# Moving the second layer's conditioning loads: two groups beside the end of the first layer's mixers, one beside the end of its FFN

## The chip, the cores and the metric

The kernel runs on one core of a Trainium2 chip. The metric is the device time of one execution in microseconds; lower is better. The engines that matter here are TensorE (PE), VectorE (DVE), ScalarE (ACT), GpSimd (POOL) and SyncE (SP), whose queue issues almost all DMAs. Every engine works through its own list of instructions in order and waits where an input or a buffer is not ready.

## The reference, cut to what matters

Two layers work on 256 context tokens and 256 latent tokens, each 1024 wide. The conditioning of a layer is one matrix product with a weight of 1024 x 6144 values:

```python
for li in range(DEPTH):                      # DEPTH = 2
    sh1, sc1, g1, sh2, sc2, g2 = split(silu(c) @ w_ada[li] + b_ada[li], 6)        # latent tokens
    sh1c, sc1c, g1c, ... = split(silu(c_ctx) @ w_ada[li] + b_ada[li], 6)          # context tokens
    p = split(modulate(x, sh1, sc1) @ w_in[li])            # input projection, 2700 columns
    mix = concat(window_attention(p), mamba2(p), diff_attention(p)) @ w_out[li]
    x = post_ln(ALPHA * x + g1 * mix)
    x = post_ln(ALPHA * x + g2 * ffn(modulate(x, sh2, sc2)))   # layer 0: SwiGLU, layer 1: 2 of 8 experts
    # context tokens: the same in layer 0; in layer 1 they only give keys, values and states
```

So of the second layer's six vectors, the first shift and scale are wanted before its input projection, the first gate and the second shift only at its output projection, and the second scale and gate after that.

## The kernel before, in words

The program is one stream of Python that emits instructions; a scheduler with its own timeline then fixes each engine's list. There are five stages: conditioning and mixers of layer 0 (to about 438 us), the FFN of layer 0 (to about 820 us), the mixers of layer 1 (to about 1086 us), routing, and the experts (from about 1120 us to the end).

**Conditioning.** `ada_group(L, g)` (from L289) computes a third of the six vectors: 2048 columns. It loads 16 pieces of 512 KB of `w_ada` (L248, called through `load_w`), and for each piece issues four matmuls of 128 x 32 by 128 x 256 (L311), which the trace records as eight, since each fp32 matmul counts twice. Below, such a piece with its matmuls is called a chunk. A group has two halves of eight chunks, and at the end of each half DVE adds the bias into the tile `rows` (L319). Group 0 then goes through two transposes into the modulation columns (L332); groups 1 and 2 write gate and shift rows to memory by DMAs in POOL's queue, `gscr<-rows` (L342).

**Buffers.** All weights outside the experts (`w_ada`, `w_in`, `w_out`, `ffn_w_down`, `ffn_w_gu`) go through one set of four buffers, the tile `raw` (`NRAW` = 4), and are issued by SP in list order. A weight that is not `w_ada` is split into a high part by ACT (`whi`, L254) and a low part by DVE or POOL (`wlo`, L255), three buffers each; its `raw` buffer is free after that. A `w_ada` buffer is free only when TensorE has read it.

**Mixers.** `mixers` weaves generators by weights and marks: the dense projection with `fill` blended into it (after `SKIP` pieces, `nfill` steps to a piece), then the output projection (`tail`); the attention streams; and the Mamba task `"S"`. A generator waits at `"?name"` until another one has yielded `"+name"`. The output projection of layer 0 is `tail0`: context tokens first, then latent tokens, `out_ab` with four sets of weights and `out_c` with two.

**Where the second layer's groups stand.** Group 0 follows the mixers of layer 0 (`for _ in ada_group(L1, 0): pass`). Groups 1 and 2 are the `fill` of the second layer's own mixers.

**End of the FFN.** The second half of the down projection has four parts, in the order `DN`: 512 columns for the context tokens, the other 512, then the same for the latent tokens. Each part takes five loads of 512 KB and one of 256 KB (tile `dn`). After a token group's second part come its layer norm, a store of the two token tiles to memory (`xscr<-xr`, L1186, in SP's queue), and the transposes `hT` that make the input of the next layer's projection (`tok` and `xbc` are the tiles of that projection).

Of the kernel before, what the change touches and what calls it, by code (L numbers as in the profile page):

```python
# [53 lines left out]
DN = ((0, CTX), (1, CTX), (0, LAT), (1, LAT))  # L54
SKIP = 11, 6
NRAW, NSPL, OT = 4, 3, 3
W1P, W2P, WCP, SYP, PRE, ADP, FUL = 1, 0, 1, 1, 1, (2, 2), 4
# [53 lines left out]
def kernel(ctx: ExitStack, tc: tile.TileContext, I, out: bass.AP):  # L111
# [57 lines left out]
    def mark(m):  # L169
        yield m  # L170
# [329 lines left out]

    def mixers(L, full_ctx, fill, tail):
        li = L.li
# [528 lines left out]
        for n in names:  # L1031
            if n == "/":
                streams.append([])
            else:
                streams[-1].append(n)
                todo.add(n)
        weave((1.0, chain(blend(dense_gen(), chain(*fill), nfill, SKIP[li]), tail)),
              *((wa[i] if type(wa) is tuple else wa, attention(n)) for i, n in enumerate(streams)), (ws, task("S")))

# [84 lines left out]

    def ffn(L, pp, done):
        li = L.li
# [27 lines left out]
        for half in range(2):  # L1154
# [8 lines left out]
            for c, tiles in ((0, (0, 1, 2, 3)), (1, (0, 1, 2, 3))) if half == 0 else DN:  # L1163
# [4 lines left out]
                for n in (2, 2, 2, 2, 2, 1):  # L1168
# [3 lines left out]
                    for t in tiles:  # L1172
                        ts_ = slice(t * 128, (t + 1) * 128)
                        mm3(pd[t], [(*(x[:, ts_] for x in act[f0 + i]), wh[:, i], wl[:, i], False) for i in range(n)],
                            f0 == 11 * half, f0 + n == 11 * half + 11)
                    f0 += n
                for t in tiles:
                    gt = gates[1 if t in CTX else 0]
                    tmp = L.pp.tile([128, 512], F, name="dtmp", tag="otmp", bufs=OT)
                    V.tensor_tensor(tmp, pd[t], gt[:, cs_], op=OP.mult)  # L1180
                    V.scalar_tensor_tensor(xs[t][:, cs_], xs[t][:, cs_], ALPHA if half == 0 else 1.0, tmp,
                                           op0=OP.mult, op1=OP.add)
                if half == 1 and c == 1:
                    for t in tiles:
                        post_ln(xs[t], g, b)
                        SP.dma_start(xscr[t * 128:(t + 1) * 128], xs[t])  # L1186
                    done(tiles)
# [509 lines left out]
    def tail0():  # L1697
# [3 lines left out]
        ns = {}  # L1701
        for tiles in TL0:
            yield from out_ab(L0, tiles, pp)
            for v in out_c(L0, tiles, pp):
# [13 lines left out]

    mixers(L0, True, [ada_group(L0, 1), ada_group(L0, 2)], tail0())
    for _ in ada_group(L1, 0):  # L1720
        pass
    with tc.tile_pool(name="ffn", bufs=1) as fp:
        ffn(L0, fp, lambda tiles: make_hT(L0.pp, L1.mod1, {t: layernorm(L0.pp, L0.xs, t) for t in tiles},
                                          tiles[0] // 2))
    post.close()
# [29 lines left out]

    mixers(L1, False, [ada_group(L1, 1), ada_group(L1, 2)], tail1())
    tail_ctx.close()
# [31 lines left out]
```

## Time and profile before

| | us |
|---|---|
| median of three runs (1867.45 to 1872.87) | 1867.92 |
| the profiled execution | 1867.13 |
| its span, first to last instruction | 1865.3 |
| PE busy, share of the span | 1712.7, 92% |
| DVE busy, share of the span | 1146.8, 61% |
| DMA, mean over the span | 234 GB/s |

The span is what the trace covers; 1.8 us of the execution lie around it. A busy PE is not a PE at its peak, since matmuls overlap and PE's clock is granted in steps. A share over the whole span says little here: the experts keep the DMA engines at 0.95 from 1120 us on, and the mixers leave them idle for tens of microseconds.

### The profile page before, as it was taken

To read this page: it belongs to the slowest core of one execution; us is meant where nothing else is said; L and a number is where in the kernel's file an instruction comes from. 1 tells how busy PE (TensorE), PEld (TensorE's weight loads), DVE (VectorE), ACT (ScalarE), POOL (GpSimd) and SP (SyncE) were. 2 spreads that over 40 slices of the span, in tenths; PEclk is the share of its full clock that TensorE was granted. 3 is DMA by queue.
4 is the path that set the end of the run, shared out by engine and by line. 5 is a ranking of instruction groups with operands and counts; after the bars stand their busy time and mean duration, and the time that the engine had idled before them with its cause. 6 is when DMAs were issued, how large, how long until landed. Compare 5 with 4: busy or idle time off the path is not lost.

```text
span 1865.3 us, 26243 instructions
## 1 busy us (share of the span) xinstructions
PE 1712.7 (92%) x9355; PEld 1262.9 (68%) x9355; DVE 1146.8 (61%) x2242; ACT 873.3 (47%) x1460; POOL 327.9 (18%) x254
## 2 busy tenths in 40 slices
PE   5889999788999999979989949999999999999995
PEld 2677667576888888857866723486458537888884
DVE  4773577768433333485777670487068408898987
ACT  3533546437322233345435721375157317777774
POOL 1221023354310222952232420000000000000000
PEclk8999999798999999998999969999999999999998
DMA  9237254158432332546672359999999999999991
GB/s 309 79 105 229 81 173 150 46 173 257 125 102 89 93 101 90 164 154 216 200 228 72 109 183 397 409 406 401 369 409 406 380 396 408 408 370 359 340 324 50
DMA packets 251002, 436.37 MB, mean 234 GB/s; under 512 B 15056, under 2 KB 166232, under 8 KB 250864
## 3 DMA queue, kind: packets, MB, share of 16 engines
q1 hardware_dynamic: 248944, 429.81, 65.1%
q0 software_dynamic: 1920, 4.81, 0.9%
q8 instruction: 76, 1.25, 0.3%
q14 instruction: 62, 0.51, 0.1%
HBM read 431.34 MB, written 3.23 MB: 233 GB/s over the span
## 4 chain that ended last, share of the span: by engine, by line
PE 75%; DMA 8%; DVE 8%; issue 3%; ACT 2%; POOL 1%; SPq 0%; DVEq 0%; ACTq 0%; POOLq 0%
PE mg L1365 6%; PE mu L1365 5%; PE mdn L1365 5%; PE gu L271 4%; PE gu L268 4%; PE gu L269 4%; DMA raw<-in_w_ada 4%; PE mg L1519 3%; PE mg L1354 3%; PE mu L1519 3%; PE mu L1354 3%; PE mdn L1354 3%; DMA mraw<-in_exp_w_down 2%; PE tok L268 2%; PE tok L271 2%
## 5 line engine op out<-in xcount | busy, mean ns | idle before, releaser
L1345 DVE TENSOR_TENSOR mwl<-mraw,mwh 128x1024 fp32r<-128x1024 f32 (+2 forms) x372 | 388.7, 1103 | 26.1 <-ACT mwh L1344 18.3
L1344 ACT ACTIVATE mwh<-mraw 128x1024 fp32r<-128x1024 f32 (+2 forms) x372 | 339.8, 965 | 84.0 <-DMA mraw<-in_exp_w_gu 45.6
L255 POOL TENSOR_TENSOR wlo<-raw,whi 128x1024 fp32r<-128x1024 f32 (+2 forms) x93 | 230.7, 2487 | 480.5 <-ACT whi L254 422.2
L254 ACT ACTIVATE whi<-raw 128x1024 fp32r<-128x1024 f32 (+2 forms) x168 | 168.3, 1004 | 239.1 <-PE dn L269 71.9
L255 DVE TENSOR_TENSOR wlo<-raw,whi 128x1024 fp32r<-128x1024 f32 (+2 forms) x75 | 88.3, 1178 | 144.2 <-ACT whi L254 142.4
L268 PE MATMUL gu<-HI,whi 128*128 128x512 f32 (+1 forms) x400 | 144.4, 369 | 2.3 <-ACT whi L254 2.3
L269 PE MATMUL gu<-LO,whi 128*128 128x512 f32 (+1 forms) x400 | 144.9, 369 | 0.0
L311 PE MATMUL ada<-raw,cT 128*32 128x256 f32 x768 | 74.8, 429 | 41.8 <-DMA raw<-in_w_ada 38.3
L268 PE MATMUL tok<-whi,HI 128*128 128x256 f32 (+2 forms) x400 | 108.0, 299 | 4.4 <-ACT xin L545 3.1
L269 PE MATMUL tok<-whi,LO 128*128 128x256 f32 (+2 forms) x400 | 105.5, 293 | 5.3 <-DVE LO L439 4.1
L271 PE MATMUL gu<-HI,wlo 128*128 128x512 f32 (+1 forms) x400 | 98.5, 367 | 0.0
L268 PEld LDWEIGHTS tok<-whi,HI 128*128 128x128 f32 x400 | 78.6, 197 | 13.5 <-issue 4.4
L268 PEld LDWEIGHTS gu<-HI,whi 128*128 128x128 f32 x400 | 75.9, 191 | 15.8 <-ACT whi L254 2.5
L269 PEld LDWEIGHTS gu<-LO,whi 128*128 128x128 f32 x400 | 76.2, 191 | 12.7
L269 PEld LDWEIGHTS tok<-whi,LO 128*128 128x128 f32 x400 | 78.5, 197 | 9.2 <-DVE LO L439 5.9
L271 PEld LDWEIGHTS gu<-HI,wlo 128*128 128x128 f32 x400 | 70.3, 188 | 12.9
L268 PE MATMUL dn<-whi,ah 128*128 128x512 f32 x176 | 70.2, 399 | 4.9 <-ACT whi L254 4.9
L1354 PE MATMUL mdn<-mwl,mah 128*128 128x512 f32 x220 | 72.8, 399 | 0.9 <-DVE mwl L1345 0.5
L1365 PE MATMUL mdn<-mwh,mah 128*128 128x512 f32 x220 | 73.5, 399 | 0.0
L1528 DVE TENSOR_TENSOR msl<-msl,mu 128x512 f32<-128x512 f32 (+1 forms) x9 | 5.8, 643 | 110.0 <-PE mu L1519 110.0
L271 PE MATMUL tok<-wlo,HI 128*128 128x256 f32 (+2 forms) x400 | 71.4, 296 | 1.9 <-DVE nw L222 1.9
L1365 PE MATMUL mdn<-mwh,mal 128*128 128x512 f32 x220 | 72.5, 394 | 0.0
(358 smaller groups left out, 3645.6 us busy)
## 6 DMA issues: line engine op xcount, KB each, us to landing
mraw<-in_exp_w_gu SPq DMA_DIRECT2D x128, 1024.0 KB, 12.4
mraw<-in_exp_w_down SPq DMA_DIRECT2D x87, 1024.0 KB, 14.5
mraw<-in_exp_w_gu SPq DMA_DIRECT2D x64, 768.0 KB, 11.4
raw<-in_w_ada SPq DMA_DIRECT2D x88, 512.0 KB, 5.4
raw<-in_ffn_w_gu SPq DMA_DIRECT2D x100, 256.0 KB, 3.3
raw<-in_w_in SPq DMA_DIRECT2D x38, 512.0 KB, 5.1
raw<-in_ffn_w_down SPq DMA_DIRECT2D x30, 512.0 KB, 3.5
E<-cscr POOLq DMA_DIRECT2D x12, 384.0 KB, 7.1
```

The costliest lines, as they stand in the source:

```text
L254: S.activation(hi, raw, AF.Copy)
L255: (eng or V).tensor_tensor(lo, raw, hi.bitcast(F), op=OP.subtract)
L268: T.matmul(o, ah, bh, start=start and i == 0, stop=False)
L269: T.matmul(o, *((ah, bl) if wa else (al, bh)), start=False, stop=False)
L271: T.matmul(o, *((al, bh) if wa else (ah, bl)), start=False, stop=stop and i == n - 1)
L311: T.matmul(pa[32 * j:32 * j + 32, hs], cT[:, k], w[j], start=(k == 0), stop=(k == KC - 1), tile_position=(0, 32 * j), skip_group_check=True)
L1344: S.activation(wh, raw, AF.Copy)
L1345: V.tensor_tensor(wl, raw, wh.bitcast(F), op=OP.subtract)
L1354: T.matmul(pc[:, :w], xh, wl[:, c * 512:c * 512 + w], start=False, stop=stop)
L1365: T.matmul(pc[:, :w], x, wh[:, c * 512:c * 512 + w], start=start and x is xh, stop=False)
L1519: T.matmul(p[hs, :n], Xf[:, kk, hs], raws[h][:, k, c * n:(c + 1) * n], start=kk == 0, stop=kk == KC - 1, skip_group_check=True)
L1528: V.tensor_tensor(sl[:, cs_], sl[:, cs_], p[:, :n], op=OP.mult)
```

## The change

`ada_group(L1, 0)` no longer stands alone after the first layer's mixers: groups 0 and 1 of the second layer are now a further generator woven into those mixers with weight 0.5, from the mark `late`, which `tail0` sets when it turns to the latent tokens. Group 2 becomes a side generator of `ffn`: one step (two chunks) after each of the five 512 KB loads of the last part of the down projection, and the rest, six chunks, before that part's layer norm. The second layer's mixers get an empty `fill`. The arithmetic is the same.

```diff
+WADA = 0.5
-    def mixers(L, full_ctx, fill, tail):
+    def mixers(L, full_ctx, fill, tail, aside=()):
...
-              *((wa[i] if type(wa) is tuple else wa, attention(n)) for i, n in enumerate(streams)), (ws, task("S")))
+              *((wa[i] if type(wa) is tuple else wa, attention(n)) for i, n in enumerate(streams)), (ws, task("S")),
+              *aside)
...
-    def ffn(L, pp, done):
+    def ffn(L, pp, done, side):
...
                     f0 += n
+                    if half == 1 and c == 1 and tiles == LAT and n == 2:
+                        next(side, None)
...
                 if half == 1 and c == 1:
+                    if tiles == LAT:
+                        for _ in side:
+                            pass
                     for t in tiles:
                         post_ln(xs[t], g, b)
...
         for tiles in TL0:
+            if tiles == LAT:
+                yield "+late"
             yield from out_ab(L0, tiles, pp)
...
-    mixers(L0, True, [ada_group(L0, 1), ada_group(L0, 2)], tail0())
-    for _ in ada_group(L1, 0):
-        pass
+
+    mixers(L0, True, [ada_group(L0, 1), ada_group(L0, 2)], tail0(),
+           [(WADA, chain(mark("?late"), ada_group(L1, 0), ada_group(L1, 1)))])
     with tc.tile_pool(name="ffn", bufs=1) as fp:
         ffn(L0, fp, lambda tiles: make_hT(L0.pp, L1.mod1, {t: layernorm(L0.pp, L0.xs, t) for t in tiles},
-                                          tiles[0] // 2))
+                                          tiles[0] // 2), ada_group(L1, 2))
...
-    mixers(L1, False, [ada_group(L1, 1), ada_group(L1, 2)], tail1())
+    mixers(L1, False, [], tail1())
```

The lists of the engines show where the chunks now stand. The first place is SP's list at the output projection of the first layer's latent tokens. Before, it holds the third and fourth set of `out_ab` weights and the two loads of `out_c`, with no `w_ada` among them:

```order
L248 DMA raw<-in_w_out 64x3x256 x2
L248 DMA raw<-in_w_out 128x256
L248 DMA raw<-in_w_out 128x2x256
L346 DMA bc<-gscr 128x1024
L248 DMA raw<-in_w_out 64x3x256 x2
L248 DMA raw<-in_w_out 128x256
L248 DMA raw<-in_w_out 128x2x256
L248 DMA raw<-in_w_out 128x2x512 x2
```

Now, from the end of the first set on:

```order
L249 DMA raw<-in_w_out 128x2x256
L249 DMA raw<-in_w_ada 128x4x256 x6
L249 DMA raw<-in_w_out 64x3x256 x2
L249 DMA raw<-in_w_out 128x256
L249 DMA raw<-in_w_out 128x2x256
L249 DMA raw<-in_w_ada 128x4x256 x3
L347 DMA bc<-gscr 128x1024
L249 DMA raw<-in_w_ada 128x4x256
L249 DMA raw<-in_w_out 64x3x256 x2
```

Six chunks have moved between the first and the second set, four between the second and the third. Before, all sixteen chunks of this stage follow the last `out_c` load; now there are thirty-two, of which eighteen stand ahead of the end of `out_c`.

The second place is SP's list at the last part of the FFN's down projection. Before:

```order
L248 DMA raw<-in_ffn_w_down 128x512
L248 DMA raw<-in_ffn_w_down 128x2x512 x3
L1186 DMA xscr<-xr 128x1024
L248 DMA raw<-in_ffn_w_down 128x2x512
L1186 DMA xscr<-xr 128x1024
L248 DMA raw<-in_ffn_w_down 128x2x512
L248 DMA raw<-in_ffn_w_down 128x512
L248 DMA raw<-in_w_in 128x4x256 x6
```

Now, from the first load of that part on:

```order
L249 DMA raw<-in_ffn_w_down 128x2x512
L249 DMA raw<-in_w_ada 128x4x256 x2
L1193 DMA xscr<-xr 128x1024
L249 DMA raw<-in_ffn_w_down 128x2x512
L1193 DMA xscr<-xr 128x1024
L249 DMA raw<-in_w_ada 128x4x256 x2
L249 DMA raw<-in_ffn_w_down 128x2x512
L249 DMA raw<-in_w_ada 128x4x256 x2
```

After three more loads with their chunks, the list goes on:

```order
L249 DMA raw<-in_ffn_w_down 128x512
L249 DMA raw<-in_w_ada 128x4x256 x6
L249 DMA raw<-in_w_in 128x4x256 x4
L1193 DMA xscr<-xr 128x1024 x2
```

Two chunks stand behind the first load and two behind each later one; the second load of the part now stands behind the first `xscr` store, where before three did not; and the first `w_in` load stands behind the last six chunks. In POOL's list the four `gscr<-rows` DMAs of group 2 now stand directly ahead of the low parts of the first `w_in` loads:

```order
L256 TENSOR_TENSOR wlo<-raw,whi 128x512
L440 TENSOR_TENSOR LO<-hfull,HI 128x256
L343 DMA gscr<-rows 2x512 x4
L256 TENSOR_TENSOR wlo<-raw,whi 128x1024 x3
L256 TENSOR_TENSOR wlo<-raw,whi 128x1072
```

The third place is TensorE's list in the second layer's mixers, at the last two state products of the Mamba task (`Sc`). Before:

```order
L814 MATMUL yoff<-Ssb,U_7547 128x192
L311 MATMUL ada<-raw,cT 32x256 x4
L767 MATMUL Sc<-xw,Bt 128x192 x2
L311 MATMUL ada<-raw,cT 32x256 x4
L747 MATMUL p_8886<-cf,U_7547 128x128 x2
L814 MATMUL yoff<-Ssb,U_7547 128x192
L311 MATMUL ada<-raw,cT 32x256 x4
L767 MATMUL Sc<-xw,Bt 128x192 x2
L311 MATMUL ada<-raw,cT 32x256 x4
L634 MATMUL tokT<-cf,qA 128x128 x3
```

Now:

```order
L748 MATMUL p_9006<-cf,U_7765 128x128 x2
L270 MATMUL tok<-whi,LO 128x256
L272 MATMUL tok<-wlo,HI 128x256 x4
L815 MATMUL yoff<-Ssb,U_7765 128x192
L635 MATMUL tokT<-cf,qA 128x128 x2
L768 MATMUL Sc<-xw,Bt 128x192 x2
L635 MATMUL tokT<-cf,qA 128x128
L786 MATMUL GT<-U_7765 128x128 x2
L815 MATMUL yoff<-Ssb,U_7765 128x192 x3
```

All `ada` rows have gone from this stage: 128 matmuls, 32 chunks. Projection matmuls stand in their place.

## Rows read from the trace of the kernel before

**Rows 1.** The page: the span, then each engine's busy time, share and instructions.

```profile
span 1865.3 us, 26243 instructions
...
PE 1712.7 (92%) x9355; PEld 1262.9 (68%) x9355; DVE 1146.8 (61%) x2242; ACT 873.3 (47%) x1460; POOL 327.9 (18%) x254
```

**Rows 2.** Stretches: us; busy PE, PEld, DVE, ACT, POOL; PE's clock; DMA share; GB/s.

```profile
350.00:380.00 30.00, 24.57 (x101) 17.14 (x100) 18.43 (x70) 16.87 (x49) 5.85 (x7) 0.72 0.00 1
380.00:410.00 30.00, 25.34 (x207) 22.79 (x206) 21.09 (x55) 9.32 (x22) 20.61 (x16) 0.94 0.55 166
410.00:440.00 30.00, 19.79 (x152) 9.93 (x151) 26.46 (x93) 12.45 (x21) 9.99 (x9) 0.86 0.98 301
```

**Rows 3.** PE in order of time, end of the first mixers; idle time in brackets.

```profile
373.27 0.87 PE L947 MATMUL py<-cf,yC 128*128 128x128 f32 x3 [3.67 <-DVE yC L937]
...
430.01 1.08 PE L311 MATMUL ada<-raw,cT 128*32 128x256 f32 x8 [1.63 <-DMA raw<-in_w_ada]
...
435.36 0.66 PE L428 MATMUL hT<-cf,lnx 128*128 128x128 f32 x4
438.31 0.58 PE L268 MATMUL gu<-HI,whi 128*128 128x256 f32 x1 [2.29 <-ACT whi L254]
```

**Rows 4.** A stretch at the end of the FFN, columns as in rows 2.

```profile
800.00:840.00 40.00, 26.68 (x145) 22.12 (x145) 35.31 (x75) 19.50 (x33) 17.91 (x10) 0.91 0.56 179
```

**Rows 5.** SP, ACT, POOL and DVE in order of time, same place.

```profile
800.76 0.34 SPq L1186 DMA_DIRECT2D xscr<-xr  x1
801.20 0.39 SPq L248 DMA_DIRECT2D raw<-in_ffn_w_down  x1
...
806.35 1.06 ACT L254 ACTIVATE whi<-raw 128x1024 fp32r<-128x1024 f32 x1 [11.21 <-DMA raw<-in_ffn_w_down]
...
785.86 12.69 POOL L255 TENSOR_TENSOR wlo<-raw,whi 128x1024 fp32r<-128x1024 f32 x5
...
790.49 3.37 DVE L228 SCALAR_TENSOR_TENSOR nw<-nwi,nw 128x1 f32<-128x1 f32 x2
...
798.81 0.35 DVE L228 SCALAR_TENSOR_TENSOR nw<-nw 128x1 f32<-128x1 f32 x2
```

**Rows 6.** POOL in order of time: the four row DMAs of group 2.

```profile
990.16 2.32 POOL L342 DMA_DIRECT2D gscr<-rows  x4 [6.78 <-DVE smx L884]
```

**Rows 7.** The `ada` matmuls alone, second mixers: stretch; busy PE, PEld, DVE.

```profile
844.00:990.00 146.00, 26.25 (x256) 7.17 (x256) 1.66 (x4) 0.94 0.68 208
```

**Rows 8.** PE in order of time, second mixers: one chunk after a wait.

```profile
952.92 0.64 PE L311 MATMUL ada<-raw,cT 128*32 128x256 f32 x8 [1.05 <-DMA raw<-in_w_ada]
```

**Rows 9.** PE's waits from 844 to 990 us: total, times, longest.

```profile
PE ada L311 <- DMA raw<-in_w_ada: 7.5, 4, 3.5
...
PE ada L311 <- DVE rows L319: 1.2, 1, 1.2
```

**Rows 10.** PE's waits from 60 to 120 us, first layer's projection.

```profile
PE xbc L268 <- ACT xin L545: 4.4, 1, 4.4
PE tok L268 <- ACT xin L545: 3.1, 1, 3.1
```

**Rows 11.** Two stretches of the second mixers, one before the experts, as in rows 2.

```profile
870.00:990.00 120.00, 110.43 (x867) 86.73 (x865) 89.35 (x225) 51.27 (x115) 33.40 (x44) 0.97 0.69 210
990.00:1072.00 82.00, 81.41 (x550) 59.74 (x550) 55.19 (x161) 52.15 (x129) 25.14 (x20) 0.98 0.26 85
1090.00:1100.00 10.00, 0.00 (x0) 0.00 (x0) 9.98 (x34) 1.06 (x1) 0.00 (x0) 0.51 1.02 413
```

## The prediction

> **What bounds the kernel now.** I read the page first. TensorE is busy for 92% of the span [rows 1], so a change that only moves TensorE's work can win no more than idle time of TensorE, and time in which its clock is low. The change adds and removes no weight load and no matmul; the second layer's three conditioning groups, 48 chunks, only change place. So I read the three places apart, by stretches, by TensorE's order of time and by its waits.
>
> At the end of the first mixers two kinds of time follow each other. From 350 to 380 us the DMA engines do nothing (share 0.00), because the four weight buffers hold output weights that wait for the last attention head; TensorE itself waits for that head, 3.67 us before 373.27. From 410 to 440 us the DMA share is 0.98 and TensorE is busy for 19.8 of 30 us: group 0 stands alone there and each chunk waits for its load [rows 2, 3]. The FFN's first matmul follows at 438.31.
>
> At the end of the FFN, from 800 to 840 us, TensorE is busy for 26.7 of 40 us, VectorE for 35.3, and the DMA engines work at 0.56 [rows 4]. What ends last there is the context tokens' layer norm: the store of its result stands in SP's list ahead of the last three down loads and is not issued before 800.76, and the load behind it, issued at 801.20, lets ScalarE go on at 806.35, after 11.21 us of idling [rows 5].
>
> In the second mixers TensorE is the bound: 110.4 busy us of 120 from 870 to 990, and 81.4 of 82 from 990 to 1072 [rows 11]. Its waits there belong to the conditioning itself, 7.5 us for `w_ada` loads and 1.2 us for the addition of the bias [rows 9].
>
> **What goes (second mixers).** 32 chunks leave. One takes 0.64 us [rows 8], which makes 20.5 us for all; their busy time together is 26.25 us [rows 7], which also counts the first part of each that lies beside the matmul before. I take the middle, 23.5. With the two waits, 8.7 us, the ceiling is 32.2. Not all of it comes back. The chunks also fill time in which the convolution needs its turn: ScalarE and VectorE must clear two `xin` buffers per piece before TensorE goes on. The first layer's projection has that piece with no chunk in it, and TensorE waits there 4.4 + 3.1 = 7.5 us [rows 10]. I charge that in full, so the stage gives back 32.2 - 7.5 = 24.7 us. The bounds are 32 (no new wait) and 9 (only the waits go, because VectorE or the Mamba chain sets the pace). The row DMAs of groups 1 and 2 also leave POOL's list in this stage [rows 6]; nothing on the path waited for them, so they count nothing.
>
> **What comes (end of the first mixers).** Group 1 is added, 16 chunks of 524,288 bytes. At the 301 GB/s that 410 to 440 us moves, a chunk costs 1.74 us of DMA and 16 cost 27.9. What takes them in: six chunks stand in SP's list between the first and second set of output weights. Three find the buffers that the loads of the second and third set fill today, and three follow as TensorE reads those, in the gap before 373.27; that is 10.4 us of loading in idle time. The price is that the second set and most of the third, 1280 KB or 4.4 us, loaded in that time today, come after. From 380 to 410 the share is 0.55, so 30 x 0.45 = 13.5 us are free; from 410 on nothing is. The FFN then begins 27.9 - 10.4 + 4.4 - 13.5 = 8.4 us later. TensorE's own part, 16 x 0.64 = 10.2 us, lies in its idle time. Bounds: 0, because the context tokens' transposes end at 435.36 + 0.66 anyway [rows 3], so the FFN cannot begin much earlier than today; and 27.9, if nothing is hidden.
>
> **What comes (end of the FFN).** Group 2, again 27.9 us of loading. Free from 800 to 840 us: 40 x 0.44 = 17.6 us. Two chunks go ahead of the first store, but in the place of two down loads, so they win nothing. The first projection weights stand behind the last six chunks, and everything that TensorE does afterwards behind them: 27.9 - 17.6 = 10.3 us late. Behind that, POOL issues the four row DMAs before it makes the low part of the first projection weights, 2.32 us [rows 6], and they wait for the last chunk. One thing helps: today POOL runs five low parts back to back from 785.86 for 12.69 us, and in that time two VectorE instructions on single columns take 3.37 us where two take 0.35 just after [rows 5]; with three down loads fewer ahead of the store the norm ends earlier, for which I take off 0.6. That makes 12 us. Bounds: below, TensorE's 10.2 us less the 13.3 that it idles in these 40 us, a gain of 3; above, 27.9 + 2.3 = 30 if nothing is hidden. I take 12 since both the free DMA time and the order of the list are read from this place itself.
>
> **Two rules of the Trainium skill, beside the sum.** The rows give 301 GB/s where conditioning weights are loaded [rows 2] and 413 where the experts' are [rows 11]. The Trainium skill, "DMA: Bandwidth & Descriptors", section "Where 436 GB/s comes from", names about 358 GB/s as what the memory gives one core; by that figure a chunk would take 1.46 us (estimate), the two additions would cost about 12.5 us together and the kernel would gain 12. Neither row is that number, one lies under it and one over, so it gets no chance of its own and I keep the 301 of the stretch that does this very work. Against the change speaks the other rule: where group 0 waits for loads today, a chunk takes 1.08 us at 430.01 and 0.64 in the second mixers [rows 3, 8], the two levels of the clock. The Trainium skill, "TensorE: Matmul & The Clock Gate", Part 1, says that bursts of matmuls between DMA waits keep the clock low; the row agrees. By that rule the first projection after the paced chunks starts at 1.2 GHz, some 2 us more. The clock is not full there today either, 0.91 from 800 to 840 [rows 4], so the sum goes without it.
>
> **The sum.** 8.4 + 12 - 24.7 = -4.3 us against the profiled execution, 1867.13 us (span 1865.3), which is 1862.8. The median of the runs shown lies 0.8 us above the profiled one, so I forecast 1863.5. What a measurement of this kernel can tell from no change is about 0.3%, 5.6 us; the forecast lies inside that.
>
> **The rivals.**
>
> *Slower: VectorE paces the second mixers.* It is busy for 89.35 of the 120 us from 870 to 990 [rows 11], and the change takes only four short additions (1.66 us) from it [rows 7]. If it, with the Mamba chain through it, cannot run above a share of 0.83, that stretch shrinks by 12 us at most, whatever TensorE gives up: 89.35 / 0.83 = 108. Then 8.4 + 12 - 12 = +8, 1876 us. It decides as soon as TensorE's new waits in the second mixers pass 15 us. For it: the 7.5 us of rows 10, at a lower load of VectorE. Against it: TensorE waits for VectorE today almost nowhere in that stretch.
>
> *Faster: the idle time takes in both groups.* The first mixers' end is bound by the context transposes rather than loads (+3), the FFN's end costs little more than half the forecast (+6), because the norm ends several us earlier and the down loads with it, and the second mixers give back 30. That is -21, 1847 us. For it: 13.3 us of idle TensorE at the FFN's end and 10.2 from 410 to 440. Against it: chunks that wait for four buffers rarely fill a DMA queue.
>
> *Slower, smaller: four buffers.* If the chunks at the two ends arrive one buffer's turn at a time, so that the first costs 14 and the second 20, the sum is +9, 1877 us. The row for it is the 5.15 us between the issue at 801.20 and the split at 806.35.
>
> That the chunks do not move is excluded by the engines' lists.
>
> **How the numbers follow.** The forecast case has 0.50; its own range is -12 to +3, that is 1856 to 1871, and about 0.21 of its 0.50 lies below -5.6. VectorE has 0.18, the idle time 0.23, the buffers 0.09. Faster by over 0.3%: 0.23 + 0.21 = 0.44. Within: 0.29. Slower: 0.18 + 0.09 = 0.27. The range reaches into both sides, from the faster case to a little past the slower ones: 1846 to 1878.
>
> **What would show it.** The FFN's first `gu` matmul at 444 to 450 us, not 438. The first steady projection matmuls about 20 us later than today, after chunks that each wait for a load. From there to the last `yC` of the second layer about 25 us less than today, with new TensorE waits on `xin` or on VectorE's tiles of under 10 us and none on `ada`. The experts' stage as long as before. The prediction is wrong if the two ends cost under 10 or over 32 us together, if the second mixers give back under 16 us, or if the experts' stage changes its length.

## The result, and the profile after

The changed kernel takes 1886.18 us (median of 11 runs, 1877.09 to 1892.55), the kernel before in the same comparison 1872.2 us (11 runs, 1863.94 to 1882.97). The ratio is 1.0077, with a 95% interval from 1.0052 to 1.0102: slower by 14 us, where 1863.5 us was forecast. The profiled execution of after took 1888.47 us.

The page of after, its span and first engines:

```profile
span 1886.7 us, 26237 instructions
...
PE 1726.5 (92%) x9355; PEld 1270.5 (67%) x9355; DVE 1153.4 (61%) x2242; ACT 876.1 (46%) x1460; POOL 323.3 (17%) x254
```

Against [rows 1] the span is 21.4 us longer with as many matmuls; TensorE is busy for 13.8 us more, at a lower mean granted clock (0.946 against 0.960 over the span). To find the place I cut both traces at seven events of TensorE's timeline: the first `op` matmul, the first and the last `gu` matmul of the FFN, the 100th and the 300th `tok` matmul behind it, the last `yC`, the first `mg` (experts). A is the end of the first mixers, F the body of the FFN, B its end, C1 and C2 the second mixers up to and from the 300th `tok` matmul, D the way to the experts.

| us | start | A | F | B | C1 | C2 | D | experts |
|---|---|---|---|---|---|---|---|---|
| before | 297.0 | 141.3 | 309.0 | 93.8 | 92.0 | 138.1 | 49.0 | 745.0 |
| after | 300.2 | 166.2 | 308.0 | 111.2 | 72.9 | 134.6 | 49.8 | 743.8 |
| forecast of the difference | 0 | +8.4 | 0 | +12 | -24.7 (C1 and C2) | | 0 | 0 |
| measured in these two profiles | +3.2 | +24.9 | -1.0 | +17.4 | -19.1 | -3.5 | +0.8 | -1.2 |

Single profiles scatter. Some kernels below have the lists of before in A (eight profiles with before's own: 140.9 to 147.9, mean 143.6) or in B (five: 93.8 to 95.3, mean 94.7). Against these means after has about +23 in A (22.6) and +16.5 in B; start, where nothing changed, is scatter.

**A.** Stretches of after, columns as in rows 2:

```profile
350.00:380.00 30.00, 23.86 (x107) 14.69 (x107) 19.68 (x89) 14.24 (x45) 5.18 (x6) 0.67 0.20 63
380.00:410.00 30.00, 26.06 (x206) 21.14 (x203) 9.04 (x29) 8.39 (x21) 11.36 (x10) 0.83 0.54 161
410.00:440.00 30.00, 22.19 (x157) 13.93 (x156) 21.50 (x80) 11.03 (x18) 14.82 (x12) 0.83 0.85 266
440.00:460.00 20.00, 12.95 (x106) 4.34 (x106) 19.34 (x61) 5.30 (x10) 6.98 (x6) 0.79 1.04 337
460.00:480.00 20.00, 16.36 (x110) 13.87 (x111) 10.38 (x13) 14.02 (x21) 11.10 (x9) 0.70 0.91 256
```

The next to last column is the one to compare with [rows 2]: from 350 to 380 us the DMA engines went from 0.00 to only 0.20, and from 380 to 410 from 0.55 to 0.54. The idle transfer time on which the forecast counted is still idle. SP's list in order of time shows why; a row's second number is the time over which its issues are spread:

```profile
348.15 29.34 SPq L249 DMA_DIRECT2D raw<-in_w_ada  x5
380.29 4.17 SPq L249 DMA_DIRECT2D raw<-in_w_out  x4
...
457.04 1.20 SPq L249 DMA_DIRECT2D raw<-in_ffn_w_gu  x2
```

Five chunk loads, the second to the sixth of the six that stand here, take from 348 to 378 us to issue, and the next output weights wait behind them. What SP waits for from 352 to 379 us (total, times, longest):

```profile
SPq L249 <- PE ada L312: 25.2, 2, 24.8
```

For 24.8 us on end SP waits until TensorE has read a chunk. TensorE's list of the same place, idle time in brackets:

```profile
374.59 2.35 PE L312 MATMUL ada<-raw,cT 128*32 128x256 f32 x24
...
379.44 0.81 PE L312 MATMUL ada<-raw,cT 128*32 128x256 f32 x8 [1.91 <-DMA raw<-in_w_ada]
382.95 1.08 PE L312 MATMUL ada<-raw,cT 128*32 128x256 f32 x8 [2.70 <-DMA raw<-in_w_ada]
385.00 1.08 PE L312 MATMUL ada<-raw,cT 128*32 128x256 f32 x8 [0.97 <-DMA raw<-in_w_ada]
386.01 0.90 PE L948 MATMUL py<-cf,yC 128*128 128x128 f32 x3
...
466.38 0.58 PE L269 MATMUL gu<-HI,whi 128*128 128x256 f32 x1 [1.25 <-ACT whi L255]
```

The first three chunks stand in TensorE's list behind the attention head and are read at 374.59, long after they were loaded. Until then their buffers are taken, so the fourth load cannot be issued. When it is, TensorE waits for it, 1.91, 2.70 and 0.97 us, with the last head's transposes (`py`, 386.01; in [rows 3] 373.27) behind. All later loads slide with SP's list, and the first `gu` weights are issued at 457.04. The whole of A, before first, then after:

```profile
297.02:438.31 141.29, 114.53 (x691) 81.02 (x690) 102.67 (x344) 69.91 (x177) 57.77 (x45) 0.86 0.50 155
```

```profile
300.20:466.38 166.18, 135.73 (x826) 87.84 (x825) 105.69 (x364) 73.12 (x180) 61.08 (x49) 0.79 0.59 188
```

TensorE is busy for 21.2 us more, and its idle time has not shrunk: 26.8 us before, 30.4 now. So on balance the added chunks did not go into idle time.

**B.** SP, ACT and POOL of after at the end of the FFN, each in order of time:

```profile
847.93 0.34 SPq L249 DMA_DIRECT2D raw<-in_ffn_w_down  x1
851.97 7.06 SPq L249 DMA_DIRECT2D raw<-in_w_ada  x6
859.91 4.94 SPq L249 DMA_DIRECT2D raw<-in_w_in  x4
...
865.65 1.06 ACT L255 ACTIVATE whi<-raw 128x1024 fp32r<-128x1024 f32 x1 [10.41 <-DMA raw<-in_w_in]
...
865.20 2.07 POOL L343 DMA_DIRECT2D gscr<-rows  x4 [9.14 <-DVE nw L229]
```

Before, the load that ACT waits for here is a down load, 11.21 us at 806.35 [rows 5]; now a second such wait has come behind it: the six chunks stand ahead of the first projection weights, and ACT idles 10.41 us for those. The four row DMAs of [rows 6] stand here as well.

**C.** The second mixers up to and from the 300th `tok` matmul, columns as in rows 2 (they replace [rows 11], which cut this stage elsewhere); before first, then after:

```profile
841.12:933.17 92.05, 89.58 (x702) 73.00 (x701) 63.22 (x169) 45.01 (x86) 25.73 (x42) 0.94 0.67 209
933.17:1071.28 138.11, 128.49 (x898) 94.74 (x896) 94.33 (x252) 75.13 (x185) 41.78 (x28) 0.96 0.45 137
```

```profile
885.57:958.47 72.90, 70.45 (x539) 67.69 (x538) 61.16 (x143) 44.57 (x88) 27.14 (x39) 0.95 0.41 113
958.47:1093.11 134.64, 124.33 (x797) 93.66 (x795) 99.77 (x249) 75.70 (x182) 33.58 (x24) 0.92 0.30 89
```

The `ada` matmuls alone in the same two stretches of before (columns as in rows 7):

```profile
841.12:933.17 92.05, 17.97 (x168) 4.96 (x168) 0.84 (x2) 0.94 0.67 209
933.17:1071.28 138.11, 8.28 (x88) 2.21 (x88) 0.83 (x2) 0.96 0.45 137
```

So before has 168 `ada` matmuls (21 chunks) in C1 and 88 (11) in C2; the expectations below, written with 20 and 12, count one too many in C2. C1 gives back 19 us, nearly one for each of its chunks; C2 gives back 3.5 us for its eleven. There 9.5 us of TensorE's waits went, 8.5 of them for the chunks, and 10.3 us of others came. TensorE's busy time fell by 4.2 us only, although 8.3 us of `ada` matmuls left, at a granted clock of 0.92 against 0.96. The longest of the new waits:

```profile
982.81 0.92 PE L815 MATMUL yoff<-Ssb,U 128*128 128x192 f32 x4 [2.82 <-DVE Ssb L779]
...
1042.03 0.66 PE L635 MATMUL tokT<-cf,kC 128*128 128x128 f32 x2 [2.49 <-DVE kC L630]
```

### The profile page after: what moved, and what is told of

Same layout as the page of the kernel before. It is cut to its first block, busy times and chain, and to the rows that moved or that the text cites. A ratio compares the mean times of both kernels' runs of the same rounds, so it can differ in the third digit from the quotient of the medians.

```text
span 1886.7 us, 26237 instructions
## 1 busy us (share of the span) xinstructions
PE 1726.5 (92%) x9355; PEld 1270.5 (67%) x9355; DVE 1153.4 (61%) x2242; ACT 876.1 (46%) x1460; POOL 323.3 (17%) x254
## 4 chain that ended last, share of the span: by engine, by line
PE 75%; DVE 9%; DMA 8%; issue 2%; ACT 2%; POOL 1%; SPq 0%; DVEq 0%; ACTq 0%
PE mg L1372 6%; PE mu L1372 5%; PE mdn L1372 5%; PE gu L269 4%; PE gu L270 4%; PE gu L272 4%; PE mg L1526 4%; DMA raw<-in_w_ada 3%; DMA mraw<-in_exp_w_down 3%; PE mu L1526 3%; PE mg L1361 3%; PE mu L1361 3%; PE mdn L1361 3%; PE tok L269 2%; PE tok L270 2%
## 5 line engine op out<-in xcount | busy, mean ns | idle before, releaser
L255 ACT ACTIVATE whi<-raw 128x1024 fp32r<-128x1024 f32 (+2 forms) x168 | 168.8, 1006 | 236.9 <-PE dn L270 72.9
L312 PEld LDWEIGHTS ada<-raw,cT 128*32 128x32 f32 x768 | 19.4, 116 | 86.2 <-DMA raw<-in_w_ada 58.6
L1372 PE MATMUL mg<-mwh,Xh 128*128 128x512 f32 x240 | 72.5, 383 | 0.0
```

Source lines behind the costliest of these rows:

```text
L255: S.activation(hi, raw, AF.Copy)
L312: T.matmul(pa[32 * j:32 * j + 32, hs], cT[:, k], w[j], start=(k == 0), stop=(k == KC - 1), tile_position=(0, 32 * j), skip_group_check=True)
L1372: T.matmul(pc[:, :w], x, wh[:, c * 512:c * 512 + w], start=start and x is xh, stop=False)
```

## The experiments

Two theories stood against each other for A. *Bytes*: 16 more loads have to pass, and what the idle time cannot hold comes on top. *Held buffers*: the loads would fit, but a chunk keeps one of the four shared buffers until TensorE comes to it in its list, so SP's list stands still and TensorE then waits for the next load. For B the theory was loads in line, against TensorE's own time. Ratios are against before, with 95% intervals. All stages in us; the last row is before, from above.

| run | median us | ratio | A | F | B | C1 | C2 |
|---|---|---|---|---|---|---|---|
| 1 first place only | 1885.57 | 1.0068 (1.0044 to 1.0091) | 176.3 | 307.8 | 95.3 | 94.4 | 132.1 |
| 2 second place only | 1894.72 | 1.0099 (1.0061 to 1.0137) | 147.5 | 308.6 | 114.1 | 90.4 | 135.6 |
| 3 loads without matmuls | 1995.30 | - | 145.4 | 309.6 | 109.1 | 69.5 | 146.8 |
| 4 matmuls without loads | 2000.16 | - | 140.5 | 315.8 | 95.5 | 78.6 | 146.0 |
| 5 own buffers | 1873.19 | 1.0014 (0.9993 to 1.0034) | 144.5 | 324.5 | 102.8 | 74.5 | 133.7 |
| 6 later at first place | 1911.69 | 1.0207 (1.0160 to 1.0255) | 182.2 | 306.8 | 111.8 | 70.8 | 143.7 |
| 7 both in FFN body | 1910.55 | 1.0209 (1.0173 to 1.0245) | 140.9 | 350.0 | 95.1 | 75.8 | 153.0 |
| 8 fill from step 10 | 1879.22 | 1.0060 (1.0036 to 1.0085) | 142.7 | 308.3 | 94.9 | 87.1 | 147.2 |
| 9 fill from step 14 | 1880.67 | 1.0037 (1.0011 to 1.0063) | 147.9 | 308.5 | 94.6 | 84.1 | 144.5 |
| 10 six chunks after FFN | 1872.97 | 1.0017 (0.9994 to 1.0040) | 142.8 | 309.6 | 98.9 | 96.2 | 128.6 |
| 11 two parts of the down | 1878.78 | 1.0047 (1.0022 to 1.0072) | 140.9 | 308.6 | 109.2 | 89.1 | 130.1 |
| 12 four parts of the down | 1906.82 | 1.0181 (1.0140 to 1.0223) | 144.4 | 308.6 | 135.1 | 80.4 | 145.4 |
| before | 1869 to 1872 | 1 | 141.3 | 309.0 | 93.8 | 92.0 | 138.1 |

**1 and 2: the two places apart.** Edits to after:

```diff
 # 1: group 2 back in the second mixers
-ada_group(L1, 2))            # side of ffn
+iter(()))
-    mixers(L1, False, [], tail1())
+    mixers(L1, False, [ada_group(L1, 2)], tail1())
 # 2: group 0 behind the first mixers as before, group 1 back
+    for _ in ada_group(L1, 0):
+        pass
+    mixers(L1, False, [ada_group(L1, 1)], tail1())
```

> Groups 0 and 1 beside the end of the first mixers as in the changed kernel, group 2 back in the second layer's own mixers, nothing at the FFN's end. In the profiles the first place cost 22 us (first attention transposes to the first gu), of which 7 could be drift of one run; the second mixers gave back 22 for two groups. If the two places are independent, this kernel stands at 22 - 11 = +11 us against before (ratio 1.006) and its FFN begins near 460 us. If the cost of the first place was mostly the one run's drift, +3 us or less. If losing the second group matters more to the second mixers than the first (TensorE's new waits come with the second), they give back 14 or more here and the sum is +8 or less.

> Group 0 alone after the first mixers as before, group 1 in the second layer's mixers, group 2 beside the FFN's end. The profiles gave 17 us for that place and half of 22 back: +6 us (ratio 1.003) with the first gu where it is before, about 438 us, if the places are independent. If the cost at the FFN's end was carried over from the late first place (lower clock), the place costs 12 us as predicted and the sum is about 0.

Each place alone costs as much as both together, by the ratios 13 and 18 us. Run 1 came near its +11, with the first `gu` at 477 us instead of 460; run 2 is beyond its +6. The table says why: with one group left, its 16 chunks all stand in C1, where before has 21, and C1 stays at 94 and 90 us; what leaves C2 is its eleven chunks, which return 2.5 to 6 us. Part of that is the clock: the granted clock of C1 is 0.89 and 0.91 in these two profiles, 0.94 before and 0.95 in after; at 0.94 the two C1 would be some 89 and 87 us (an estimate from these figures). So runs 1 and 2 do not show that sixteen chunks cost as much in C1 as 21. The two places are independent of each other (B is 95.3 without the second place, A 147.5 without the first).

A of run 1, with the lists of after, is 10 us longer than A of after, at a granted clock of 0.74 against 0.79. The profiled execution of run 1 took 1901.28 us, 16 above its median, that of after 2 above; so I go by after for the size of A.

**3 and 4: loads without matmuls, matmuls without loads.** Edits to after:

```diff
 # 3: of eight chunks of a half, only the last is multiplied
-                for j in range(4):
+                for j in range(4) if not li or k == KC - 1 else ():
...
 # 4: one load per group
+                    if not li or h + k == 0:
                         t = load_w([(None, src)], [128, 4, 256], pool)
```

> As the changed kernel, all 48 loads of the second layer's conditioning weights, but 14 of 16 chunks of a group have no matmuls (their products are left out); such a buffer is free as soon as its load has landed. Theory bandwidth: the loads alone set the time, the first place stays at +20 us and the FFN's end at +15. Theory buffers (a chunk holds one of four until TensorE reads it): the first place falls to about +8, the FFN's end to about +8, since a buffer's turn becomes the load alone. Theory TensorE's list (chunks that wait for loads stand ahead of the last attention head and of the output projection): the first place falls to +3 or less, though the same bytes are loaded.

> As the changed kernel, all matmuls of the second layer's conditioning in place, but each group loads one chunk of 16 and multiplies it 16 times (the other 15 loads are left out). Theories bandwidth and buffers: both places lose their cost; the first gu comes at or ahead of the time of before, about 430 to 440 us, and the FFN's end costs 10 us of TensorE's work less its idle time, 0 to 3. Theory TensorE's list: the chunks still stand there but wait for nothing, so only 32 x 0.64 = 20 us of TensorE in time that idles today, and the same outcome as the other two; what differs is then only the loads-only run. If a cost of over 10 us stays here at the first place, none of the three holds and the cost is TensorE's own time at the low clock.

With other conditioning the tokens are routed otherwise and the experts run over 100 us longer, so both are read only up to C2. At the first place each half of the work alone is free: 145.4 and 140.5 us, about the range of before (in run 4 eight chunks' products have slid into F, which is 7 us longer). All 32 loads fit into the stage when a buffer is free as soon as its load has landed. SP's list and two stretches of run 3:

```profile
347.82 7.20 SPq L249 DMA_DIRECT2D raw<-in_w_ada  x5
357.26 2.38 SPq L249 DMA_DIRECT2D raw<-in_w_out  x4
361.24 19.48 SPq L249 DMA_DIRECT2D raw<-in_w_ada  x4
...
438.53 7.64 SPq L249 DMA_DIRECT2D raw<-in_ffn_w_gu  x6
```

```profile
350.00:380.00 30.00, 22.19 (x89) 13.91 (x88) 20.53 (x76) 15.21 (x48) 8.21 (x7) 0.72 0.52 157
380.00:410.00 30.00, 24.36 (x179) 22.98 (x179) 14.33 (x65) 10.20 (x23) 13.55 (x11) 0.88 0.61 193
```

The same five issues are through in 7 us instead of 29, the output weights follow at 357 instead of 380, the transfers use 0.52 of a stretch that had 0.20, and the `gu` weights are issued at 438.53 instead of 457.04. So the cost of A hangs on neither the bytes nor the products alone, but on a load's buffer waiting for TensorE's turn. *Bytes* alone falls. How the cost divides between SP's list standing still and TensorE waiting at a chunk whose load is late is not shown: in run 3 both are gone (TensorE's waits on chunk loads in A are 1.8 us, 17.4 in after), and its A, 2 us above the mean of before, is what the expectation named for the second (+3 or less), not for the buffers (+8). At the FFN's end the two halves part: loads alone cost 109.1 - 94.7 = 14 us, products alone 1 us. There it is the loads in line.

**5: two more buffers, for the second layer's chunks alone.** Edit to after (the three groups pass `"post0"`; the normalised rows `lnx` have two buffers instead of four, for room):

```diff
+OWN = 2
...
-        raw = (pool or wp).tile(shape, F, name="raw", tag="raw", bufs=LRB if pool else NRAW)
+        if pool == "post0":
+            pool = L0.pp
+        raw = (pool or wp).tile(shape, F, name="raw", tag="raw", bufs=(LRB if pool is lp else OWN) if pool else NRAW)
```

> As the changed kernel, but the second layer's conditioning weights have two buffers of their own beside the four that all other weights share (the normalised rows have two buffers instead of four, to make room). With the room the lists change too: about 16 of the 32 chunks of the first place now stand behind the FFN's first loads. Theory buffers (the shared four, held by chunks that wait for TensorE, keep the output weights back): the way from the first op matmul to the first gu falls from 166 to 176 us to 150 or less, against 141 to 147 without the change, and the kernel comes to before or below it (ratio 0.997 to 1.002). Theory TensorE's list (a chunk that waits for its load blocks the attention head and the output projection behind it, whoever owns the buffer): with only two buffers each chunk waits longer, the first place stays over 160 us or the FFN takes the wait over (gu to last gu over 315 us instead of 309), ratio 1.006 or more.

The slowdown is gone (1.0014, the interval includes 1), but not because the first place takes the chunks in: its idle time stays idle (DMA 0.17 and 0.57 in the two stretches of above). The list changes. Chunk loads and `gu` loads no longer want the same buffers, so fifteen chunks stand among the first `gu` weights, one beside two of those, where F pays 15.5 us for them. Part of the expectation holds (A 144.5), part of its rival too (F over 315). With one chunk more than before in A (17 instead of 16), the run does not test what own buffers are worth there.

**6: fewer chunks ahead of the output weights.** Edit to after:

```diff
-WADA = 0.5
+WADA = 0.12
```

> As the changed kernel with the weight of the new generator at 0.12 instead of 0.5: same buffers, same bytes, same matmuls, but only six of the 32 chunks stand ahead of the last output weights instead of eighteen; the others stand where group 0 stood before. Theory coupling (chunks among the output weights hold buffers and TensorE's place in line): the output projection ends about as before, the loads that are left, 26 chunks at 1.74 us = 45 us less the 10 us of group 0 that were hidden before, come at the end instead; the first op to the first gu takes 141 to 147 + 6 to 18 us. If it were simply bytes that have to be loaded ahead of the FFN, the way is as long as with 0.5: 166 to 176 us, ratio 1.008. If the position among the output weights is the cost, 150 to 158 us and a ratio of 1.000 to 1.004.

The expectation failed: A is 182.2 us. SP and TensorE in order of time:

```profile
457.36 17.59 SPq L249 DMA_DIRECT2D raw<-in_w_ada  x6
...
468.65 0.69 PE L333 MATMUL tp<-cf,rows 128*128 128x128 f32 x2 [0.22 <-ACT hfull L436]
...
470.94 3.33 PE L312 MATMUL ada<-raw,cT 128*32 128x256 f32 x32 [0.69 <-DVE rows L320]
475.82 0.64 PE L312 MATMUL ada<-raw,cT 128*32 128x256 f32 x8 [1.54 <-DMA raw<-in_w_ada]
477.92 1.08 PE L312 MATMUL ada<-raw,cT 128*32 128x256 f32 x8 [1.46 <-DMA raw<-in_w_ada]
```

None of the three theories came out; they named 147 to 176 us. SP's list stands still again, at another spot: four chunks are loaded, but stand in TensorE's list behind the context rows' transposes and the conversion of group 0 (`tp`), and are read at 470.94. Until then no further chunk load is issued, and afterwards each of the last chunks waits for a load of its own. Neither position tried here was free; what both have in common is that TensorE has other work ahead of chunks that are already loaded.

**7: both groups in the FFN's body.** Edit: group 0 as before, and after each step of the second half's gate and up projection two steps of groups 1 and 2:

```diff
                 gate_up(f, slice(0, 2))
+                if half == 1:
+                    for _ in range(2):
+                        next(side, None)
```

> Group 0 as before; groups 1 and 2 stand in the second half of the FFN's gate and up projection, four chunks to a step, where the DMA engines work at 0.32 to 0.39 and TensorE is the bound; the second mixers have no chunk, as in the changed kernel. It prices the second mixers without the two ends. TensorE's work there is 32 x 0.57 to 0.64 = 18 to 20 us more from the first to the last gu (309 us before), if no chunk waits for its load; more if four buffers make TensorE wait there too (over 25). If the second mixers give back 22 as in the changed kernel's profile: sum -4 to 0, ratio 0.998 to 1.000. If they give back 25 or more: 0.996. If they give back under 10, because what counted in the changed kernel was not the fill but where the stage was cut: +10 us, ratio 1.005.

F grows by 41 us, 1.28 for a chunk, although the DMA engines work there at 0.28 to 0.33 without them (before, 592 to 747 us). TensorE's groups from 592 to 792 us (busy time, then idle time before them):

```profile
L269 PE MATMUL gu<-HI,whi 128*128 128x512 f32 x176 | 74.5, 424 | 15.2 <-ACT whi L255 15.2
```

Four chunks in a row, as many as there are buffers, stand ahead of the next `gu` weights, and TensorE idles 15.2 us for those; the products take some 20 us (32 x 0.64), and its clock is 0.94 and 0.91 in the two stretches with chunks (640 to 760 us), 1.00 just before. The second mixers gave back only 1 us here, not 22: C2 is 153 us (last section).

**8 and 9: the fill of the kernel before, later.** Edits to before:

```diff
-SKIP = 11, 6
+SKIP = 11, 10      # run 9: 11, 14
```

> The kernel before with one number changed: the fill of the second layer's mixers begins after 10 projection steps instead of 6, so about 15 of its 32 chunks move from the first part of that projection (up to the 300th tok matmul) to the second. The profiles so far: without any chunk the first part is 92 - 73 = 19 us shorter, which had 20 chunks; the second part 138 - 134 = 4 us, which had 12. Theory place (chunks in the second part lie in time in which TensorE waits for VectorE and the Mamba chain anyway, in the first part TensorE is the bound): the first part gives back about 12 of its 19 us and the second takes 2 to 6 more, sum -6 to -10, ratio 0.995 to 0.997. Theory of the prediction (a chunk costs TensorE's 0.64 us wherever it stands in these mixers): no change, 0.999 to 1.001. Rival: chunks in the second part hold buffers and wait for their loads as before (8.5 us of such waits there), so more of them there cost more: 1.002 or above.

> As the run before, with the fill after 14 steps: 12 chunks now stand behind the whole projection, beside the attention heads. Theory place: -8 to -14 us for the first part, +4 to +8 for the second, ratio 0.995 to 0.998; it turns above 1 if the last chunks, whose gates the output projection needs, arrive late there (group 2's rows are wanted only at the second norm, group 1's at the output projection). Theory 0.64 us wherever: 0.999 to 1.001.

Both expectations of a gain are wrong. C1 gives back 5 and 8 us, C2 takes 9 and 6, and the kernels are slower by 0.6 and 0.4%; the granted clock of C2 is 0.91 and 0.92, 0.96 before. In run 9 the way to the experts, D, is also longer, 53.5 us instead of 49.0. That eleven chunks of C2 returned little does not mean that more of them are free there.

**10: the six chunks away from the first projection weights.** Edit to run 2: `side` is not drained in `ffn`, what is left of it heads the fill:

```diff
-                    if tiles == LAT:
-                        for _ in side:
-                            pass
...
-    mixers(L1, False, [ada_group(L1, 1)], tail1())
+    mixers(L1, False, [side, ada_group(L1, 1)], tail1())
```

> As the run with the second place only, but the last six chunks of group 2 stand in the second mixers' fill, ahead of group 1, instead of ahead of the FFN's last norm and the first projection weights. Theory loads in line (their six loads keep the first projection weights back; the profile with loads and hardly any matmuls had the FFN's end at 109 us against 95 with the matmuls and hardly any loads, 111 to 114 with both, 94 to 95 with none): the FFN's end falls from 114 to 97 to 103 us, the second mixers take 6 x 0.64 = 4 us more, ratio 1.003 to 1.007 against before instead of 1.010. Theory TensorE's time: the end falls by 4 us only and the mixers take 4 more: ratio 1.010 again.

B falls from 114.1 to 98.9 us and the ratio from 1.0099 to 1.0017. Its rows, for comparison with B of after:

```profile
824.12 0.34 SPq L249 DMA_DIRECT2D raw<-in_ffn_w_down  x1
826.41 14.64 SPq L249 DMA_DIRECT2D raw<-in_w_in  x8
...
830.25 1.06 ACT L255 ACTIVATE whi<-raw 128x1024 fp32r<-128x1024 f32 x1 [0.57 <-DMA raw<-in_w_in]
```

The projection weights follow the last down load at once, and ACT waits 0.57 us instead of 10.41. So of B's cost the six chunks in line are 12 to 15 us, their products (6 x 0.64) among it, the other ten 4.

**11 and 12: more chunks among the down loads.** Edits to run 10, with `side` made of groups 1 and 2:

```diff
-                    if half == 1 and c == 1 and tiles == LAT and n == 2:
+                    if half == 1 and tiles == LAT and n == 2:     # run 12: len(tiles) == 2 for tiles == LAT
```

> Group 0 as before. Groups 1 and 2 go two chunks at a time behind the loads of both last parts of the FFN's down projection (20 chunks instead of the 10 of the run before), the remaining 12 stand in the second mixers' fill, none ahead of the first projection weights in a row. From the stages measured: ten chunks in the last part cost the FFN's end 98.9 - 94.7 = 4 us and a chunk in the first part of the second mixers costs about 1 us (92 - 73 = 19 us for 20 chunks). Theory (a chunk costs only TensorE's time there as long as its load finds free DMA time and nothing waits behind it): 10 more cost 4 to 6 us at the FFN's end and save 8 to 10 in the mixers; against before -2 to -6, ratio 0.997 to 0.999. Rival: the part before has TensorE at full clock and no idle time, and its chunks make it wait for loads, as the FFN's gate and up projection did (1.28 us a chunk): +13 and -10, ratio 1.002 to 1.004.

> As the run before with all four parts of the second half's down projection: all 32 chunks stand there, two behind each 512 KB load, and the second mixers have none. Each such step then loads 1.5 MB, 5 us at 301 GB/s, beside some 5 us of TensorE's products. If the loads keep up: 32 x 0.6 = 19 us more there against 20 to 23 us that the mixers give back, ratio 0.997 to 1.000. If four shared buffers make TensorE wait there as in the gate and up projection (1.28 us a chunk): +41 - 22, ratio 1.010. The stages tell them apart: from the last gu to the 100th tok matmul 113 to 118 us or 130 and more, against 95.

The rivals hold at the FFN's end: 109.2 and 135.1 us in B. Run 11 has 18 chunks in B where run 10 has ten, and the eight more cost 10.3 us; the 32 of run 12 cost 40 us. That is 1.26 to 1.29 us for a chunk, as in the FFN's body. In run 12 the mixers gave back 4 us instead of 22 (C1 80.4, C2 145.4), so the ratio is 1.018 and not 1.010. No version beats the kernel before; runs 5 and 10 equal it within their intervals.

## Why the prediction was wrong, point by point

**The end of the first mixers: +8.4 forecast, about +23 measured; this is the step that failed.** Its sentences were that three chunks "follow as TensorE reads those, in the gap before 373.27; that is 10.4 us of loading in idle time", and that "from 380 to 410 the share is 0.55, so 30 x 0.45 = 13.5 us are free". Transfer time that was idle was counted as usable. It is idle because the buffers hold weights for which TensorE's list has not come round yet, and chunks behind the same list do not change that: the share went to 0.20 and 0.54. The first three chunks found buffers, as forecast; the other three were to follow in the gap before 373.27, but TensorE read the first chunk only at 374.59, behind the last head's products, and SP waited 24.8 us for it. With 63 GB/s for 30 us, 3.6 chunks or 6.3 us were loaded early; 27.9 - 6.3 = 21.6 us remain, close to the measured 23. That sum is made after the fact and leaves out the 4.4 us that the prediction charged for output weights. A chunk's 1.74 us was not far off: the 337 GB/s from 440 to 460 us make it 1.56. The sentence that TensorE's 10.2 us lie in its idle time failed as well: that time went from 26.8 to 30.4 us. The prediction had this mechanism as its smallest rival (*Slower, smaller: four buffers*, 14 at A and 20 at B, a chance of 0.09, 1877 us), and the argument that chunks which wait for four buffers rarely fill a DMA queue stands in it against the rival *Faster*. It came out, dearer at A and cheaper at B than its price.

**The end of the FFN: +12 forecast, +16.5 measured.** The mechanism was right: the six loads ahead of the first projection weights. They cost 12 to 15 us (run 10) where 10.3 was forecast, and the ten others 4 where the free transfer time was to hide them. The four row DMAs on POOL take 2.07 us as forecast, but begin while ACT still waits for weights (865.20 against 865.65); the rows of B show both. The norm does end earlier, and by more than the 0.6 us that were taken off: the first store is issued 49.0 us behind the last `gu` matmul instead of 53.5 (823.44 - 774.40 against 800.76 - 747.29), with two down loads fewer ahead of it, not three. So the 4 us of the ten chunks are what is left after that gain.

**The second mixers: -24.7 forecast, -22.6 measured.** The size is right in these two profiles, its make-up is not, and as other profiles without chunks give back between 1 and 23 us (last section), the size is in part luck. No wait of 7.5 us for `xin` came; the waits that are not for chunks went from 2.8 to 12.7 us in small pieces, the longest for VectorE (`yoff`, `tokT`). The rival *VectorE paces the second mixers* came out in part in C2, which shrank by 3.5 of the 16 to 17 us that its chunks took with their waits, but VectorE is busy for 0.74 of it only; in C1 its share rose to 0.84 (61.16 of 72.90 us), over the 0.83 that the rival took for its limit.

**The clock.** The prediction left out of its sum the loss of clock through chunks paced by their loads. At A it came: from 451.37 us to the first `gu` a chunk takes 1.06 to 1.08 us after waits for its load, where those from 440 to 449 us take 0.64, and the granted clock of A is 0.79 against 0.86. What it cost there is not shown: from 440 us on the DMA engines are at 0.91 to 1.04, so the chunks wait for loads at either clock. At B the chunks after waits of 0.6 to 0.95 us (859 to 864 us) still take 0.64, but the clock falls right behind the last of them, and the first projection matmuls run at the lower level. TensorE's list there, and the stretch, columns as in rows 2:

```profile
863.78 0.64 PE L312 MATMUL ada<-raw,cT 128*32 128x256 f32 x8 [0.95 <-DMA raw<-in_w_ada]
866.76 0.58 PE L269 MATMUL tok<-whi,HI 128*128 128x256 f32 x1 [2.35 <-ACT whi L255]
```

```profile
864.47:871.29 6.82, 4.53 (x21) 4.53 (x22) 6.80 (x19) 3.84 (x4) 5.75 (x6) 0.50 0.87 294
```

At half the clock its 4.53 busy us cost about 2.3 (estimate), the 2 us that the prediction named and left out; before, the clock is low for 3.4 us at this point too. The Trainium skill, "TensorE: Matmul & The Clock Gate", Part 1, says of short bursts of matmuls between DMA waits that the wait throttles the engine and the next burst starts at the low clock; both places agree with that.

**What was right.** Experts and FFN body kept their length, no wait on `ada` is left in the second mixers, and the new waits there are 9.9 us, just under the 10 that were named. The first `gu` matmul came at 466.38 us, not at the 444 to 450 that were to show the change. The mark of being wrong was named: two ends that cost over 32 us together. They cost about 39.

## What to carry to other kernels

Idle time of the DMA engines is not room for more loads unless something frees a buffer in it: look at what holds the buffers and when its reader's list comes to it, and count only the buffers that come free in the idle stretch. A chunk that was moved for spare bandwidth alone blocked the issuing list until its reader came to it, and then the reader until the next load had landed. And price a removal stage by stage, with the granted clock beside it: 21 chunks were worth 19 us in one half of a stage and eleven 3.5 us in the other, so that each half of the change alone was as dear as the whole.

## What was not expected of the hardware

Second mixers without any chunk lose TensorE's clock in some profiles. The wait of 2.8 us ahead of `yoff`, shown above for C, comes in all of them, but what follows differs. The stretch around it in after, and in run 7, columns as in rows 2:

```profile
978.00:998.00 20.00, 15.95 (x71) 10.49 (x71) 15.28 (x43) 6.86 (x20) 4.67 (x4) 0.74 0.34 92
```

```profile
983.00:1003.00 20.00, 16.02 (x54) 10.43 (x55) 12.78 (x36) 6.76 (x19) 3.71 (x3) 0.63 0.34 92
...
1063.00:1083.00 20.00, 18.21 (x76) 13.55 (x76) 8.18 (x20) 11.56 (x26) 3.90 (x3) 0.59 0.54 186
```

In run 7 the clock falls a second time from 1063 us. Over the whole of C2 the granted clock was 0.92 in after and 0.93 in run 5, and 0.82 to 0.86 in runs 3, 4, 6, 7 and 12; C2 took 134 to 135 us in the first two and 144 to 153 in the others, with 797 to 802 matmul records each. So what the mixers give back lies between 1 and 23 us in these profiles, and the clock after such waits goes with it. What decides between the two I did not settle. Before, whose chunks stand in that time, has 0.96 there.
